# A two-layer block on one Trainium2 core: the delta rule's inverse in blocks of 64, and four other moves in the order of the work

## The chip, the core and the metric

The kernel runs on one core of one Trainium2 chip. The metric is the device time of one execution in microseconds (us), lower is better. Before the change three runs took 820.45, 818.7 and 819.86 us; the median is 819.86 us.

## What is computed

Two layers are applied to x of shape (1, 256, 1024) in fp32. The first holds a Mamba-2 branch (SSD), an RG-LRU branch and a feed-forward part with a depthwise convolution; the second has four branches (gated delta rule, spatial gating, sliding window, attention to a memory of 256 tokens), each gated and projected up. The parts that the change touches are these, cut from the reference:

```python
# RG-LRU gates, 16 blocks of 64 channels
r = sigmoid(einsum("bshi,hij->bshj", xb, wr) + br)
i = sigmoid(einsum("bshi,hij->bshj", xb, wi) + bi)
# memory branch: the memory is normed, then projected to keys and values
mem_kv = _rmsnorm(mem, norm_mem) @ w_mem_kv
# delta rule: q and k with unit length, 4 heads of 128
q = _l2norm(q) * (DN_DK ** -0.5); k = _l2norm(k)
L = where(strict, einsum("bhncd,bhnsd->bhncs", kb, k) * exp(diff), 0.0)
sol = triangular_solve(eye + L, rhs, left_side=True, lower=True, unit_diagonal=True)
```

The reference solves in chunks of 64 tokens; the kernel works in chunks of 128, so that there are 2 chunks x 4 heads = 8 unit triangular matrices of 128 x 128 to be inverted.

## The kernel before

**Products.** All activations lie with channels or tokens on the 128 partitions, 256 tokens wide. Every fp32 weight comes from HBM in pieces of 128 x 1024 (512 KB) that SyncE's queue streams through three raw buffers. ScalarE rounds a piece to `whi` (L112), VectorE computes the rest `wlo` (L113), and TensorE makes each product from three matmuls: high by high, low by high, high by low (`mm3`, L419 to L421; `proj_wide`, L457). In the first products of all, `ly`, the activations themselves are also being split while they are used: `HU` on ScalarE (L616), `LU` on VectorE (L617).

**The order.** TensorE, ScalarE and VectorE run what the program's order gives them. Class `Weave` (L146) makes the order: a main generator walks through the big projections and yields after each small unit of matmuls; side generators hold everything else. A side's `yield n` asks for n units of the main work before it goes on, `yield ("event", n)` asks for n units after a named event, and a plain string in the main work joins a side: what is left of it is then emitted at once. In the first layer's gate and merge projections a unit is 3 x 2 matmuls of 128x512. TensorE executes strictly in that order, so whatever is placed too early makes TensorE wait. Instructions inside `tc.high_priority()` are moved ahead on ScalarE and VectorE.

**Places that the change touches.**
- The LRU gates `pg` (L804): after part p of the projection `lx` the convolution leaves `XC`; half of it, the channels of the odd blocks, is copied by a DMA of GpSimd's queue to `XW` (L1030) so that all blocks lie on partitions 0 to 63. The gates of part p are issued 10 units after `lx{p}`.
- The memory (`prm`, L924): the norms of the memory tokens are spread over the partitions by two matmuls, ScalarE copies them to `MEM` (L927), GpSimd scales the transposed memory `MT` in four operations (L932), ScalarE rounds each half to `EH` (L934), VectorE makes the rest `EL` (L935). All that runs beside the projections `pb` and `o`; `m1b` (L962) transposes the merged branches into `MH` and `ML` (L965, L966), which `o` reads.
- The norms of q and k (`pss`, L1270; `psst`, L1279): two sets of matmuls, with a copy `ss` on VectorE (L1274) between them.
- The inverse. `diagonal()` (from L1238) sends the 32 x 32 diagonal blocks through a DRAM tensor `dl` so that they lie with (matrix, block) on the partitions, and GpSimd does the forward substitution for 32 blocks at once: 31 steps of a product (L1250) and a subtraction (L1254), 128 x 248 elements in the first and 128 x 8 in the last. The results go back through `dx`. Then, 44 units later, two levels of merges on TensorE turn blocks of 32 into 64 and 64 into 128: per level and chunk four matmuls `pit` (L1344), four transposes `piy` (L1353) and four matmuls `pix` (L1362, L1364).
- `delta` is joined by the main work just before the merge of branch 3; `G2` (gates of a branch) and `MG2` (their sum) have separate buffers.

Of the kernel before, what the change touches and what calls it, by code (L numbers as in the profile page):

```python
# [8 lines left out]
F32 = mybir.dt.float32  # L9
# [187 lines left out]
def two_blocks_kernel(  # L197
# [11 lines left out]
    lvl: bass.AP,  # L209
# [153 lines left out]
    def small_proj(o, hh, hl, a, n, nm):  # L363
# [9 lines left out]
        nc.vector.tensor_copy(f, pf[:, 0:S])  # L373
        yield 5
# [8 lines left out]
    def rows(o, src, nm, wait):  # L383

        n = src.shape[2]
        cat = sm.tile([P, 2, P], F32R, tag="cat", name=f"{nm}_cat", bufs=1)
        nc.gpsimd.memset(cat.bitcast(F32), 0.0)
        split(cat[:, :, 0:n], cat[:, :, n : 2 * n], src)
# [4 lines left out]
        nc.vector.tensor_copy(o, pT[:, 0:S])  # L393
# [508 lines left out]
    def side_mem():  # L902
# [18 lines left out]
        yield 8  # L921
# [23 lines left out]
    class Merged:  # L945
# [11 lines left out]
        def turn(self, tt, c):  # L957
            yield 4 if self.nm == "m1" else 3
# [177 lines left out]
    def block2(HH, HL, HX, MK, MV):  # L1136
        lws = big.tile([P, 16, P], F32, tag="b8", name="lws")
        wst = lws[:, 0:4, :]
        lvs = lws[:, 4:9, :].rearrange("p a c -> p (a c)")
        lv = lvs[:, 0:448].rearrange("p (l c) -> p l c", l=7)  # L1140
        lv0 = lvs[:, 448:576]
# [10 lines left out]
        nc.sync.dma_start(lvs[:, 0:576], lvl)  # L1152
# [17 lines left out]
        XI = [bXY[:, 0], bXY[:, 1]]  # L1170
        YI = [bXY[:, 2], bXY[:, 3]]

# [10 lines left out]
        def side_decay():  # L1183
# [3 lines left out]
            nc.scalar.activation(beta, ba[:, :, 0:4], AF.Sigmoid)  # L1187
            nc.vector.tensor_tensor(
                out=gg, in0=ba[:, :, 4:8],
                in1=row("dt_bias_2").unsqueeze(1).to_broadcast([P, 2, 4]), op=ALU.add)  # L1190
            ggf = gg.rearrange("p t h -> p (t h)")
            softplus(ggf, ggf, 8, "spdn")
            nc.vector.scalar_tensor_tensor(
                gg, in0=gg, scalar=-1.0, in1=ea2.unsqueeze(1).to_broadcast([P, 2, 4]),
                op0=ALU.mult, op1=ALU.mult)
# [4 lines left out]
            nc.vector.tensor_copy(gc, pgc[:, 0:12])  # L1200
            gcT = sm.tile([P, S], F32R, name="gcT", bufs=1)
            nc.vector.tensor_tensor(out=kds, in0=gc[:, 8:12], in1=gc[:, 0:4], op=ALU.subtract)
            nc.scalar.activation(kds, kds, AF.Exp)
            nc.scalar.activation(e1, gc[:, 4:8], AF.Exp)
            nc.vector.tensor_scalar(neg1, e1, -1.0, None, op0=ALU.mult)
            yield from rows(gcT, gc[:, 0:8].rearrange("p (c h) -> p c h", c=2), "pgT", 9)
            yield 2
            for c in range(2):
# [5 lines left out]
                for h in range(4):  # L1214
                    nc.scalar.activation(EE[c][:, h, :], pe[:, h * P : (h + 1) * P], AF.Relu,
                                         scale=-1.0, bias=gc[:, 4 * c + h : 4 * c + h + 1])
                nc.scalar.activation(EE[c], EE[c], AF.Exp, scale=-1.0)
# [3 lines left out]
                yield 1  # L1221

        sqs = {}

        def diagonal():

            LA8 = bLA[:, 0:2].rearrange("p c h l -> p (c h) l")
            XI8 = bXY[:, 0:2].rearrange("p c h l -> p (c h) l")
            dl = dp.tile([8, 4, 32, 32], F32, name="dl")
            dx = dp.tile([8, 4, 32, 32], F32, name="dx")  # L1230

            lb = bXY[:, 2:4].rearrange("p a h (b l) -> p (a h b) l", l=32)
            xb = bM[:, 0:256].rearrange("p (i k) -> p i k", k=8)
            ta = bM[:, 256:512].rearrange("p (i k) -> p i k", k=8)
            eng = nc.gpsimd
            for b in range(4):
                r = slice(32 * b, 32 * b + 32)
                eng.dma_start(dl[:, b].rearrange("c s l -> s c l"), LA8[r, :, r])  # L1238
            eng.memset(XI8, 0.0)
            eng.memset(xb, 0.0)  # L1240
            for g in range(4):
                q = slice(32 * g, 32 * g + 32)
                eng.affine_select(out=xb[q], in_=xb[q], compare_op=ALU.not_equal, fill=1.0,
                                  base=-8 * g, pattern=[[1, 32], [-1, 8]],
                                  channel_multiplier=0)
                eng.dma_start(lb[q], dl.rearrange("c b s l -> (c b) s l"))
            for j in range(31):
                n = 31 - j
                t = ta[:, 0:n, :]
                eng.tensor_tensor(  # L1250
                    out=t, in0=xb[:, j : j + 1, :].to_broadcast([P, n, 8]),
                    in1=lb[:, j, j + 1 : 32].unsqueeze(2).to_broadcast([P, n, 8]),
                    op=ALU.mult)
                eng.tensor_tensor(out=xb[:, j + 1 : 32, :], in0=xb[:, j + 1 : 32, :], in1=t,  # L1254
                                  op=ALU.subtract)
            for g in range(4):
                eng.dma_start(
                    dx[:, :, :, 8 * g : 8 * g + 8].rearrange("c b i k -> (c b) i k"),
                    xb[32 * g : 32 * g + 32])
            for b in range(4):  # L1260
                r = slice(32 * b, 32 * b + 32)
                eng.dma_start(XI8[r, :, r], dx[:, b].rearrange("c i k -> i c k"))

        def side_delta():

            for a in range(2):
                yield (f"dn{a}1", 10)
                pss = bank(f"pss{a}")
                for h in range(4):
                    nc.tensor.matmul(pss[32 * h : 32 * h + 32, 0:S], one[:, 0:32],  # L1270
                                     sqs[a, h // 2][:, h % 2, :], start=True, stop=True,
                                     tile_position=(0, 32 * h))
                f = sm.tile([P, S], F32, tag="spf", name=f"ss{a}", bufs=1)
                nc.vector.tensor_copy(f, pss[:, 0:S])  # L1274
                yield 3
                pst = bank(f"psst{a}")
                for tt in range(2):
                    t = slice(tt * P, (tt + 1) * P)
                    nc.tensor.transpose(pst[:, t], f[:, t], ident)  # L1279
                nc.vector.tensor_copy(  # L1280
                    rn[:, a], pst[:, 0:S].rearrange("p (t h c) -> p t h c", t=2, c=32)[:, :, :, 0])


            sk, rq = rn[:, 0], rn[:, 1]
            nc.scalar.activation(sk, sk, AF.Sqrt, bias=eps1)
            nc.scalar.activation(rq, rq, AF.Sqrt, bias=epsq, scale=128.0)
            nc.vector.reciprocal(rq, rq)
            nc.vector.reciprocal(wk, sk)
            nc.vector.tensor_tensor(out=wk, in0=wk, in1=wk, op=ALU.mult)
            nc.vector.tensor_tensor(out=wk, in0=wk, in1=beta, op=ALU.mult)  # L1290
# [13 lines left out]
            yield 1  # L1304
# [3 lines left out]
            for c in range(2):  # L1308
                t = slice(c * P, (c + 1) * P)
                for p in range(2):  # L1310
# [5 lines left out]
                    for j in range(2):  # L1316
                        h = 2 * p + j
                        nc.vector.scalar_tensor_tensor(
                            LT[c][:, h, :], in0=pk[:, j * S : j * S + P],
                            scalar=wk[:, c, h : h + 1], in1=EE[c][:, h, :],  # L1320
                            op0=ALU.mult, op1=ALU.mult)
                    e = EE[c][:, 2 * p : 2 * p + 2, :]
                    nc.vector.tensor_tensor(out=e, in0=v2(pk)[:, :, P:S], in1=e, op=ALU.mult)
# [3 lines left out]


            diagonal()
            yield 44  # L1330

            def even(ap, l):
                return ap.rearrange("p (b a i) -> p b a i", a=2, i=1 << l)[:, :, 0, :]

            def even4(ap, l):
                return ap.rearrange("p h (b a i) -> p h b a i", a=2, i=1 << l)[:, :, :, 0, :]

            Ts = [None, None]
            for l in range(5, 7):
                for c in range(2):  # L1340
                    pt = bank(f"pit{l}{c}")
# [570 lines left out]
```

## Time and profile before

| | |
|---|---|
| runs | 818.7, 819.86, 820.45 us (median 819.86) |
| the profiled execution | 822.88 us, of which the span from its first to its last instruction is 821.2 us |
| TensorE (PE) busy | 804.1 us, 98% of the span; mean granted clock 0.997 |
| VectorE (DVE) busy | 612.9 us, 75% |
| ScalarE (ACT) busy | 526.8 us, 64% |
| GpSimd (POOL) busy | 67.5 us, 8% |
| DMA | 147.63 MB, 180 GB/s over the span |

The profile is of one execution, which took 3.0 us longer than the median of the runs. Engines run side by side, so that the busy shares do not add up; the chain of work that ended last says which of them set the end, and the list of waits says where TensorE stood still. "a x4" in a row stands for four instructions in a row of the same kind; an fp32 product that is not split shows as two matmuls in the trace, so that "x8" are four products.

### The profile page before, as it was taken

How to read it: one execution, taken by the hardware profiler on the slowest of the kernel's cores; microseconds unless marked ns; L12 is line 12 of the kernel's file. 1: busy time of each engine (PE TensorE's matmuls, PEld its weight loads, DVE VectorE, ACT ScalarE, POOL GpSimd, SP SyncE). 2: the span in 40 equal slices, each digit the busy share in tenths (PEclk: the TensorE clock that was granted, in tenths of full speed). 3: DMA queues.
4: the chain of work that ended last, by engine and by line, in shares of the span. 5: the costliest groups of instructions: out<-in, count | busy, mean ns of one | idle time of the engine just before them, and what ended most of it. 6: DMA issues, size and time to landing. Idle time of an engine off the chain costs nothing.

```text
span 821.2 us, 13190 instructions
## 1 busy us (share of the span) xinstructions
PE 804.1 (98%) x4978; PEld 708.2 (86%) x4978; DVE 612.9 (75%) x1017; ACT 526.8 (64%) x830; POOL 67.5 (8%) x113
## 2 busy tenths in 40 slices
PE   6999999899999999999999999999999999999997
PEld 6999887688879999999988889888888888888886
DVE  5899799888688788888744687877786657566583
ACT  7585998895656656565644378955976555544452
POOL 0000001000200000000000100029830000000000
PEclk9999999999999999999999999999999999999999
DMA  8655456466754655555566554543554445655651
GB/s 317 204 206 172 133 168 209 152 217 229 262 171 135 222 188 180 185 175 198 195 199 201 185 166 146 188 150 107 175 148 148 137 145 169 194 192 190 199 185 52
DMA packets 41631, 147.63 MB, mean 180 GB/s; under 512 B 5024, under 2 KB 5280, under 8 KB 41568
## 3 DMA queue, kind: packets, MB, share of 16 engines
q1 hardware_dynamic: 40464, 144.82, 52.3%
q0 software_dynamic: 960, 1.97, 1.1%
q8 instruction: 39, 0.64, 0.3%
q14 instruction: 24, 0.20, 0.1%
q10 hardware_dynamic: 144, 0.00, 0.0%
HBM read 144.42 MB, written 1.31 MB: 177 GB/s over the span
## 4 chain that ended last, share of the span: by engine, by line
PE 92%; DVE 5%; DMA 2%; ACT 1%; issue 0%; DVEq 0%; SPq 0%; ACTq 0%; POOLq 0%
PE z L457 8%; PE fu L421 6%; PE fu L420 6%; PE fu L419 6%; PE g L419 5%; PE g L420 5%; PE g L421 5%; PE fd L421 3%; PE fd L420 3%; PE fd L419 3%; PE lx L457 2%; PE up L421 2%; PE up L419 2%; PE up L420 2%; PE o L421 1%; PE xbc L419 1%
## 5 line engine op out<-in xcount | busy, mean ns | idle before, releaser
L113 DVE TENSOR_TENSOR wlo<-wraw,whi 128x1024 fp32r<-128x1024 f32 x256 | 312.6, 1227 | 132.3 <-ACT whi L112 129.6
L112 ACT CAST whi<-wraw 128x1024 fp32r<-128x1024 f32 x256 | 267.3, 1050 | 192.0 <-PE fu L420 48.1
L419 PE MATMUL fu<-HX,whi 128*128 128x256 f32 x384 | 108.7, 283 | 0.0
L420 PE MATMUL fu<-HX,whi 128*128 128x256 f32 x384 | 108.7, 283 | 0.0
L421 PE MATMUL fu<-HX,wlo 128*128 128x256 f32 x384 | 108.7, 283 | 0.0
L419 PE MATMUL g<-whi,HX 128*128 128x512 f32 x192 | 76.3, 397 | 0.0
L420 PE MATMUL g<-wlo,HX 128*128 128x512 f32 x192 | 75.3, 392 | 0.0
L421 PE MATMUL g<-whi,HX 128*128 128x512 f32 x192 | 75.2, 392 | 0.0
L419 PEld LDWEIGHTS fu<-HX,whi 128*128 128x128 f32 x384 | 73.7, 192 | 0.0
L420 PEld LDWEIGHTS fu<-HX,whi 128*128 128x128 f32 x384 | 73.7, 192 | 0.0
L421 PEld LDWEIGHTS fu<-HX,wlo 128*128 128x128 f32 x384 | 73.7, 192 | 0.0
L457 PE MATMUL z<-HX,whi 128*128 128x512 f32 x192 | 69.7, 400 | 0.0
L457 PE MATMUL z<-HX,wlo 128*128 128x256 f32 x192 | 51.3, 288 | 0.0
L599 DVE SCALAR_TENSOR_TENSOR fc<-fu,pc,fc 128x255 f32<-128x255 f32 (+1 forms) x96 | 43.7, 478 | 1.6
L419 PEld LDWEIGHTS g<-whi,HX 128*128 128x128 f32 x192 | 36.3, 189 | 8.6 <-issue 1.1
L421 PEld LDWEIGHTS g<-whi,HX 128*128 128x128 f32 x192 | 36.3, 189 | 7.7
L420 PEld LDWEIGHTS g<-wlo,HX 128*128 128x128 f32 x192 | 36.4, 189 | 7.2
L457 PEld LDWEIGHTS z<-HX,whi 128*128 128x128 f32 x192 | 35.6, 188 | 6.4 <-issue 0.3
L457 PEld LDWEIGHTS z<-HX,wlo 128*128 128x128 f32 x192 | 36.3, 189 | 2.1 <-issue 0.5
L419 PE MATMUL fd<-whi,FH 128*128 128x512 f32 x96 | 37.4, 389 | 0.0
L420 PE MATMUL fd<-wlo,FH 128*128 128x512 f32 x96 | 37.4, 389 | 0.0
L421 PE MATMUL fd<-whi,FL 128*128 128x512 f32 x96 | 37.3, 389 | 0.0
(533 smaller groups left out, 1890.4 us busy)
## 6 DMA issues: line engine op xcount, KB each, us to landing
wraw<-in_w_in_dram SPq DMA_DIRECT2D x130, 512.0 KB, 3.4
wraw<-in_w_fu_dram SPq DMA_DIRECT2D x48, 512.0 KB, 3.6
wraw<-in_w_fd_dram SPq DMA_DIRECT2D x24, 512.0 KB, 3.6
wraw<-in_w_o_dram SPq DMA_DIRECT2D x16, 512.0 KB, 4.1
wraw<-in_w_up_dram SPq DMA_DIRECT2D x16, 512.0 KB, 3.3
wraw<-in_w_pa_dram SPq DMA_DIRECT2D x8, 512.0 KB, 4.1
wraw<-in_w_pb_dram SPq DMA_DIRECT2D x8, 512.0 KB, 4.3
wraw<-in_w_mk_dram SPq DMA_DIRECT2D x4, 512.0 KB, 4.4
```

What stands on the lines that cost most here:

```text
L112: nc.scalar.copy(hi, raw)
L113: nc.vector.tensor_tensor(out=lo, in0=raw, in1=hi.bitcast(F32), op=ALU.subtract)
L419: nc.tensor.matmul(o, wh, xh, start=first, stop=False)
L420: nc.tensor.matmul(o, wh, xl, start=False, stop=False)
L421: nc.tensor.matmul(o, wl, xh, start=False, stop=last)
L457: nc.tensor.matmul(*p, start=k + i == 0, stop=k == 7 and i == 1)
L599: nc.vector.scalar_tensor_tensor(o[:, d:S], in0=p[:, 0 : S - d], scalar=col(wname, (taps - 1 - d) * n + i), in1=o[:, d:S], op0=ALU.mult, o ...
```

## The change

1. **Blocks of 64.** `diagonal()` goes. GpSimd now inverts the 16 diagonal blocks of 64 x 64 (`unit`, `blocks_out`, `rows_in`, `forward`, `blocks_in`): 63 steps of a product and a subtraction, on 128 partitions that hold (column residue mod 8, block). The first 16 of these operations are on one column group of up to 63 elements, the longest are on 128 x 156. Rows of the blocks come in four portions of eight DMAs on GpSimd's own queue, placed among the steps. One merge is left on TensorE: 8 transposes of 64 x 64 (`pix0`), 8 products of 64 x 64 (`pit`), 8 more (`pix1`), with copies on ScalarE and VectorE between. It is due 72 units after the event `inv`. The table `lvl` and its DMA go.
2. **The norms apart.** The norm of k comes first (`norms(0)`, 10 units after `dn01` as before), that of q after the blocks have been handed to GpSimd. The products k·k and k·q (`pkk`) no longer wait for `dn21`. Short VectorE and ScalarE operations of this side work run with high priority.
3. **Products on zeros.** VectorE clears 128 x 384 elements of `NRM` at the very start, and six 128x256 fp32 products on them (`pw`) stand ahead of TensorE's first work.
4. **Memory.** `prm` is due 15 units instead of 8 after the norms, `m1` takes a unit less between its pieces.
5. **LRU gates.** `pg` is due 12 units after `lx{p}` instead of 10.
6. **Buffers.** `G2` of branch 3 is summed in place, the other branches' `G2` lies in buffer `b3`, `delta` is joined one branch later.

```diff
-            yield (f"lx{p}", 10)
+            yield (f"lx{p}", 12)
...
-        yield 8
+        yield 15
         ps = bank("prm")
...
-            yield 4 if self.nm == "m1" else 3
+            yield 3
...
+        def rows_in(i):
+            for g in range(8):
+                q, r = slice(16 * g, 16 * g + 16), slice(16 * i, 16 * i + 16)
+                if i < 2:
+                    o, c = lb0[q, r], slice(0, 64)
+                else:
+                    o, c = lb1[q, 16 * i - 32 : 16 * i - 16], slice(32, 64)
+                nc.gpsimd.dma_start(o, dl[:, :, r, c].rearrange("c b s l -> (c b) s l"))
+        def forward(js):
+            eng = nc.gpsimd
+            for j in js:
+                a, n = j // 8 + 1, 63 - j
+                t = bM[:, 1792 : 1792 + a * n].rearrange("p (k i) -> p k i", k=a)
+                l = lb0[:, j, j + 1 : 64] if j < 32 else lb1[:, j - 32, j - 31 : 32]
+                eng.tensor_tensor(
+                    out=t, in0=xb[:, 0:a, j : j + 1].to_broadcast([P, a, n]),
+                    in1=l.unsqueeze(1).to_broadcast([P, a, n]), op=ALU.mult)
+                x = xb[:, 0:a, j + 1 : 64]
+                eng.tensor_tensor(out=x, in0=x, in1=t, op=ALU.subtract)
...
-            for a in range(2):
-                yield (f"dn{a}1", 10)
...
+            yield ("dn01", 10)
+            yield from norms(0)
...
+            yield ("E", 1)
+            yield ("dn11", 6)
...
+            blocks_out()
+            rows_in(0)
+            forward(range(4))
+            rows_in(1)
+            forward(range(4, 16))
+            wv.event("inv")
+            yield from norms(1)
...
+            yield ("inv", 8)
+            forward(range(16, 20))
+            rows_in(2)
+            forward(range(20, 32))
+            rows_in(3)
+            forward(range(32, 63))
+            blocks_in()
             yield ("dn21", 7)
...
-            diagonal()
-            yield 44
...
+            yield ("inv", 72)
+            X0 = bXY[0:64, 0:2].rearrange("p c h l -> p (c h l)")[:, 0:512]
+            T = tmp("T")[64:P]
+            px = bank("pix0")
+            for i in range(8):
+                nc.tensor.transpose(px[0:64, i * 64 : (i + 1) * 64], YI8[0:64, i, 0:64],
+                                    ident[0:64, 0:64])
+            nc.scalar.copy(X0, px[0:64])
+            yield 3
...
-                yield "delta"
-                MG = big.tile([P, 2, D], F32, tag="b3", name="MG2")
+                MG = G2
...
             elif n == 2:
+                yield "delta"
...
+            nc.vector.memset(NRM[:, 0:384], 0.0)
+            pw = bank("pw")
+            for _ in range(6):
+                nc.tensor.matmul(pw[:, 0:S], NRM[:, 0:P], NRM[:, P : P + S], start=True, stop=True)
```

How the change moves instructions shows at three places. The first is TensorE around the last part's LRU gates `pg`, beside the gate projection `g`; `pg` from `XW` is what needs the copied half. Before, `pg` follows the first two units of `g`'s column block `g_00_1776`:

```order
L419 MATMUL g_00_1776<-whi_1670,HX_102 128x512
L420 MATMUL g_00_1776<-wlo_1671,HX_102 128x512
L421 MATMUL g_00_1776<-whi_1670,HX_102 128x512
L804 MATMUL pg_1796<-XC,lw 64x256
L804 MATMUL pg_1797<-XW,lw 64x256
```

After the change the same gates (`pg_1843`, `pg_1844`) stand behind twelve more matmuls of `g` and behind the eight small `pgr`:

```order
L586 MATMUL pgr<-ident2r,gnrh 128x128
L588 MATMUL pgr<-ident2r,gnrl 128x128
L421 MATMUL g_10_1785<-whi_1678,HX_102 128x512
L422 MATMUL g_10_1785<-wlo_1679,HX_102 128x512
L423 MATMUL g_10_1785<-whi_1678,HX_102 128x512
L421 MATMUL g_10_1785<-whi_1678,HX_102 128x512
L422 MATMUL g_10_1785<-wlo_1679,HX_102 128x512
L423 MATMUL g_10_1785<-whi_1678,HX_102 128x512
L806 MATMUL pg_1843<-XC,lw 64x256
L806 MATMUL pg_1844<-XW,lw 64x256
```

So `pgr`, which came after the gates, now comes before them, and the gates come twelve matmuls and these eight later.

The second place is ScalarE in the projection `o`, where `EH` is the rounded scaled memory, `MH` the rounded merged branches, and `whi` a rounded weight piece. Before, eight `EH` stand ahead of the last two `MH`, which `o` needs at once:

```order
L965 CAST MH<-m1b_2360 128x4x128
L112 CAST whi_2412<-wraw_2336 128x1024
L927 COPY MEM<-prm 128x256
L112 CAST whi_2418<-wraw_2342 128x1024
L965 CAST MH<-m1b_2403 128x4x128
L934 ACTIVATE EH<-MT,pc 128x256 x8
L554 ACTIVATE warm<-eps_99 128x1
L112 CAST whi_2460<-wraw_2410 128x1024
L112 CAST whi_2466<-wraw_2416 128x1024
L965 CAST MH<-m1b_2482 128x4x128
L112 CAST whi_2510<-wraw_2458 128x1024
L965 CAST MH<-m1b_2501 128x4x128
```

After the change:

```order
L112 CAST whi_2450<-wraw_2400 128x1024
L967 CAST MH<-m1b_2460 128x4x128
L929 COPY MEM<-prm 128x256
L936 ACTIVATE EH<-MT,pc 128x256 x3
L967 CAST MH<-m1b_2503 128x4x128
L936 ACTIVATE EH<-MT,pc 128x256 x5
L112 CAST whi_2518<-wraw_2442 128x1024
L112 CAST whi_2524<-wraw_2448 128x1024
```

The last `MH` now stands behind three `EH` only; the weight pieces `whi_2518` and `whi_2524` of `o`'s second half stand behind all eight.

The third place is GpSimd at the start of the inverse: the blocks go out to `dl`, come back as rows, and the steps begin. Before:

```order
L1238 DMA dl<-bLA 32x8x32 x4
L1246 DMA bXY<-dl 32x1024 x4
L1250 TENSOR_TENSOR bM<-bM,bXY 128x248
L1254 TENSOR_TENSOR bM<-bM 128x248
L1250 TENSOR_TENSOR bM<-bM,bXY 128x240
L1254 TENSOR_TENSOR bM<-bM 128x240
```

After the change:

```order
L1258 DMA dl<-bLA 64x8x64 x2
L1268 DMA lb_5143<-dl 16x1024 x10
L1277 TENSOR_TENSOR bM<-bM,lb_5143 128x63
L1268 DMA lb_5143<-dl 16x1024
L1281 TENSOR_TENSOR bM<-bM 128x63
L1268 DMA lb_5143<-dl 16x1024
L1277 TENSOR_TENSOR bM<-bM,lb_5143 128x62
L1268 DMA lb_5143<-dl 16x1024
L1281 TENSOR_TENSOR bM<-bM 128x62
```

Ten row DMAs are issued ahead of the first step, and one more between each two operations until all are out; the steps are shorter in the beginning and there are twice as many.

## Rows read from the trace of the kernel before

**Rows 1.** The page, the chain that ended last, shares of the span by engine.
```profile
PE 92%; DVE 5%; DMA 2%; ACT 1%; issue 0%; DVEq 0%; SPq 0%; ACTq 0%; POOLq 0%
```
**Rows 2.** Waits of TensorE: line and releaser, us in total, times, longest.
```profile
PE pg L804 <- DMA XW<-XC: 2.1, 1, 2.1
PE o L421 <- DVE ML L966: 1.1, 1, 1.1
PE psst L1279 <- DVE ss L1274: 0.9, 1, 0.9
```
**Rows 3.** Timeline of TensorE, the start: start us, duration us, instruction, [idle before].
```profile
6.71 0.58 PE L419 MATMUL ly<-HU,whi 128*128 128x256 f32 x1 [6.71 <-ACT HU L616]
...
10.81 0.38 PE L421 MATMUL ly<-HU,wlo 128*128 128x256 f32 x1
11.03 0.29 PE L419 MATMUL ly<-HU,whi 128*128 128x256 f32 x1
...
19.08 0.68 PE L628 MATMUL prx<-ident,rx 128*128 128x128 f32 x4
```
**Rows 4.** Timeline of VectorE, the operation that makes prx's operand.
```profile
18.78 0.16 DVE L1764 RECIPROCAL rx<-rx 128x2 f32<-128x2 f32 x1
```
**Rows 5.** Timeline of TensorE at the last part's LRU gates.
```profile
146.70 0.40 PE L804 MATMUL pg<-XW,lw 64*64 64x256 f32 x1 [2.06 <-DMA XW<-XC]
```
**Rows 6.** Busy time by stretch behind these gates (PE, PEld, DVE, ACT, POOL, PEclk, DMA).
```profile
148.00:150.00 2.00, 2.00 (x5) 1.48 (x5) 1.18 (x3) 1.98 (x5) 0.00 (x0) 0.50 0.73 252
```
**Rows 7.** The chain at these gates, in order of time: start us, us, what.
```profile
141.94 4.63 DMA XW<-XC
...
146.70 1.59 PE pg L804 x12
...
149.02 0.43 PE g L420
```
**Rows 8.** Timeline of TensorE, the memory norms.
```profile
218.99 0.60 PE L924 MATMUL prm<-ident,rm 128*128 128x128 f32 x4
```
**Rows 9.** Timeline of GpSimd, the scaling of the memory.
```profile
220.59 7.17 POOL L932 TENSOR_TENSOR MT<-MT,MEM 128x512 f32<-128x512 f32 x4 [77.62 <-ACT MEM L927]
```
**Rows 10.** Timeline of ScalarE, the last two roundings of the memory.
```profile
227.79 0.91 ACT L934 ACTIVATE EH<-MT,pc 128x256 fp32r<-128x256 f32 x2 [0.52 <-POOL MT L932]
```
**Rows 11.** The chain at the merges, in order of time.
```profile
625.27 0.84 PE pit L1344 x8
626.11 0.44 PE piy L1353 x4
626.55 2.79 PE z L457 x16
...
642.42 0.60 PE pit L1344 x8
643.02 0.59 PE piy L1353 x4
...
652.84 0.23 PE g L420
```
**Rows 12.** Timeline of TensorE, the last products k·k and k·q.
```profile
541.07 1.03 PE L1314 MATMUL pkk<-KQ 128*128 128x256 f32 x4
```
**Rows 13.** Timeline of GpSimd: three steps of the substitution, and the way back.
```profile
557.30 0.70 POOL L1254 TENSOR_TENSOR bM<-bM 128x240 f32<-128x240 f32 x1
...
561.65 1.53 POOL L1254 TENSOR_TENSOR bM<-bM 128x216 f32<-128x216 f32 x1
...
596.24 0.20 POOL L1250 TENSOR_TENSOR bM<-bM,bXY 128x8 f32<-128x8 f32 x1
...
605.02 2.33 POOL L1262 DMA_DIRECT2D bXY<-dx  x4 [4.89 <-DMA dx<-bM]
```
**Rows 14.** Timeline of VectorE beside the second of these steps.
```profile
561.35 1.31 DVE L113 TENSOR_TENSOR wlo<-wraw,whi 128x1024 fp32r<-128x1024 f32 x1
```

More of the change, by code (lines that the diff above doesn't have):

```diff
@@ L372, in small_proj @@
         f = sm.tile([P, S], F32, tag="spf", name=f"{nm}_f", bufs=1)
-        nc.vector.tensor_copy(f, pf[:, 0:S])
-        yield 5
+        with tc.high_priority():
+            nc.vector.tensor_copy(f, pf[:, 0:S])
+        yield 3
         ps = bank(f"{nm}t")
@@ L387, in rows @@
         nc.gpsimd.memset(cat.bitcast(F32), 0.0)
-        split(cat[:, :, 0:n], cat[:, :, n : 2 * n], src)
+        with tc.high_priority():
+            split(cat[:, :, 0:n], cat[:, :, n : 2 * n], src)
         yield wait
@@ L392, in rows @@
             nc.tensor.transpose(pT[:, tt * P : (tt + 1) * P], cat[:, tt].bitcast(F32), ident)
-        nc.vector.tensor_copy(o, pT[:, 0:S])
+        with tc.high_priority():
+            nc.vector.tensor_copy(o, pT[:, 0:S])
     def softplus(o, v, n, nm):
@@ L1186, in side_decay @@
             yield from small_proj(ba, HH, HL, baab[0], 8, "psb")
[L1187 to L1195, printed above, removed]
+            with tc.high_priority():
+                rates()
             yield 9
@@ L1199, in side_decay @@
             nc.tensor.matmul(pgc[:, 8:12], one, gg[:, 0, :], start=True, stop=True)
-            nc.vector.tensor_copy(gc, pgc[:, 0:12])
+            with tc.high_priority():
+                nc.vector.tensor_copy(gc, pgc[:, 0:12])
             gcT = sm.tile([P, S], F32R, name="gcT", bufs=1)
[L1202 to L1206, printed above, removed]
+            yield from rows(gcT, gc[:, 0:8].rearrange("p (c h) -> p c h", c=2), "pgT", 5)
             yield 2
@@ L1213, in side_decay @@
                                      gcT[:, c * P : (c + 1) * P], start=True, stop=True)
[L1214 to L1217, printed above, removed]
+                with tc.high_priority():
+                    for h in range(4):
+                        nc.scalar.activation(
+                            EE[c][:, h, :], pe[:, h * P : (h + 1) * P], AF.Relu,
+                            scale=-1.0, bias=gc[:, 4 * c + h : 4 * c + h + 1])
+                    nc.scalar.activation(EE[c], EE[c], AF.Exp, scale=-1.0)
                 nc.gpsimd.affine_select(
@@ new lines, in block2, with unit @@
+        sqs = {}
+        dl = dp.tile([8, 2, 64, 64], F32, name="dl")
+        dy = dp.tile([8, 2, 64, 64], F32, name="dy")
+        lb0 = big.tile([P, 32, 64], F32, tag="b1", name="lb0")
+        lb1 = bXY[:, 0:2].rearrange("p c h (a l) -> p (c h a) l", l=32)
+        def unit():
+            eng = nc.gpsimd
+            eng.memset(YI8, 0.0)
+            eng.memset(xb, 1.0)
+            for sign in (1, -1):
+                eng.affine_select(
+                    out=xb, in_=xb, compare_op=ALU.is_ge, fill=0.0,
+                    base=15 if sign > 0 else 0, pattern=[[-128 * sign, 8], [16 * sign, 64]],
+                    channel_multiplier=-sign)
@@ L1235, in diagonal, with blocks_out @@
+        def blocks_out():
+            LA8 = bLA[:, 0:2].rearrange("p c h l -> p (c h) l")
             eng = nc.gpsimd
-            for b in range(4):
-                r = slice(32 * b, 32 * b + 32)
+            for b in range(2):
+                r = slice(64 * b, 64 * b + 64)
                 eng.dma_start(dl[:, b].rearrange("c s l -> s c l"), LA8[r, :, r])
[L1239 to L1246, printed above, removed]
@@ new lines, in blocks_in, with norms @@
+        def blocks_in():
+            eng = nc.gpsimd
+            for g in range(8):
+                eng.dma_start(
+                    dy.rearrange("c b (k g) i -> g (c b) k i", g=8)[g],
+                    xb[16 * g : 16 * g + 16])
+            for b in range(2):
+                r = slice(64 * b, 64 * b + 64)
+                eng.dma_start(YI8[r, :, r], dy[:, b].rearrange("c k i -> k c i"))
+        def norms(a):
+            pss = bank(f"pss{a}")
+            for h in range(4):
+                nc.tensor.matmul(pss[32 * h : 32 * h + 32, 0:S], one[:, 0:32],
+                                 sqs[a, h // 2][:, h % 2, :], start=True, stop=True,
+                                 tile_position=(0, 32 * h))
+            f = sm.tile([P, S], F32, tag="spf", name=f"ss{a}", bufs=1)
+            with tc.high_priority():
+                nc.vector.tensor_copy(f, pss[:, 0:S])
+            yield 3
+            pst = bank(f"psst{a}")
+            for tt in range(2):
+                t = slice(tt * P, (tt + 1) * P)
+                nc.tensor.transpose(pst[:, t], f[:, t], ident)
+            with tc.high_priority():
@@ L1303, in side_delta @@
                                         op=ALU.mult)
[L1304 to L1310, printed above, removed]
-                    pk = bank(f"pkk{c}{p}")
-                    for j in range(2):
-                        h = 2 * p + j
-                        nc.tensor.matmul(pk[:, j * S : (j + 1) * S], KQ[:, h, 0, t],
-                                         KQ[:, h, :, t], start=True, stop=True)
[L1316 to L1323, printed above, removed]
-                    yield 1
@@ new lines, in side_delta @@
+                yield 1
+            yield ("inv", 72)
[6 more added lines that the diff above has]
+            nc.scalar.copy(X0, px[0:64])
+            yield 3
+            pt = bank("pit")
+            for i in range(8):
+                nc.tensor.matmul(pt[64:P, i * 64 : (i + 1) * 64], LT[i // 4][0:64, i % 4, 64:P],
+                                 X0[:, i * 64 : (i + 1) * 64], start=True, stop=True)
@@ L1377, in solve @@
+            nc.scalar.activation(T, pt[64:P], AF.Copy, scale=-1.0)
+            yield 3
+            px = bank("pix1")
+            for i in range(8):
+                nc.tensor.matmul(px[0:64, i * 64 : (i + 1) * 64], T[:, i * 64 : (i + 1) * 64],
+                                 YI8[64:P, i, 64:P], start=True, stop=True)
+            nc.vector.tensor_copy(YI8[0:64, :, 64:P],
+                                  px[0:64].rearrange("p (c l) -> p c l", c=8))
+            yield 3
             def solve(c):
@@ L1697, in block2 @@
                 wv.add("y0", branch0())
-            G2 = big.tile([P, 2, D], F32, tag="b1", name=f"G2{n}")
+            G2 = big.tile([P, 2, D], F32, tag="b1" if n == order[0] else "b3", name=f"G2{n}")
             for c in range(2):
@@ L1788 @@
 _ARGS = (
[L1789 removed]
+    "x", "xT", "mem", "memT", "pcol", "prow", "wsm", "lruw", "wsT", "post", "gbias", "w_in", "w_pa", "w_pb",
     "w_o", "w_mk", "w_mv", "w_fu", "w_fd", "w_in2", "w_up2", "w_o2",
@@ L1879, in _layout @@
     d["wsT"] = np.ascontiguousarray(a("spatial_w_2")[0].transpose(2, 0, 1)).reshape(P, 4 * P)
-    i = np.arange(P)
-    lv = []
-    for l in range(7):
-        b = i >> l
-        m = np.where((b[:, None] % 2 == 1) & (b[None, :] == b[:, None] - 1), -1.0, 0.0)
-        lv.append(m[:, b % 2 == 0])
-        if l == 0:
-            m0 = m.T
-    d["lvl"] = np.concatenate(lv + [m0], axis=1).astype(np.float32)
     return {k: np.ascontiguousarray(d[k]) for k in _ARGS}
```

136 lines of the change are left out of this document (47 added, 89 removed).

## The prediction

> **What bounds the kernel now.** I read the chain that ended last first: TensorE holds 92% of it [rows 1], so a change counts only where TensorE waits, runs at half clock, or is given less to do. The list of its waits comes next. Beside the unavoidable start it holds three that the change touches: 2.1 us for the copied half `XW` of the LRU gates, 1.1 for `ML` in `o`, 0.9 for the copy `ss` in the norms [rows 2]. Then the timelines at these places, for what a wait costs beyond itself, and the chain at the merges, for the work that falls away. Everything below is a difference to the profiled execution of 822.88 us, which lies 3.0 above the median of 819.86; I take the differences off the median. About 0.2%, or 1.6 us, is what a measurement of this kernel can tell from no change.
>
> **LRU gates, -4.1 us.** The last gates stand still for 2.06 us until 146.70 [rows 5], because the DMA to `XW` was issued at 141.94 and needs 4.63 us, landing at 146.57 [rows 7]. It is not only that: behind the wait the granted clock falls to 0.50, the lower level of 1.2 GHz [rows 6]. The twelve gate records take 1.59 us and a matmul of `g` 0.43 [rows 7], where one at full clock takes 0.23 [rows 11]. Six of them pass before the clock is back, 6 x 0.20 = 1.2, and the gates themselves lose about half, 0.8. Wait and clock are 4.1 us. After the change the gates come behind twelve more matmuls of `g`, 12 x 0.23 = 2.8 us, and behind the eight `pgr`. Without the wait the first that reads `XW` would have run at 146.70 - 2.06 = 144.6; now it is due at 147.4, and some 0.8 later still for `pgr`. `XW` lands at 146.57 if its producer is not moved, so 0.8 to 1.6 us are to spare. What hides it is `g`, whose weights are already split by then. Bounds: nothing if `XC` comes two microseconds later, 4.3 if all goes.
>
> **Memory and `o`, -0.3 us.** The 1.1 us for `ML` [rows 2] go, since only three `EH` stand ahead of its `MH` on ScalarE. No clock fell behind this wait. But something else is now late: `whi_2518` and `whi_2524` stand behind all eight `EH`, and these are paced by GpSimd's four scalings, 7.17 us [rows 9]. In the trace the last `EH` is done 227.79 + 0.91 - 218.99 = 9.7 us after `prm` [rows 8, 10]. The piece of weight then needs a rounding and a subtraction, 1.0 and 1.3 us [rows 14] (that row is a subtraction; the rounding takes a little less), so its low half is there 11.6 us after `prm`, with some overlap 11.3. In the new order 43 matmuls of `o` at 0.23 and the last `m1b` stand between `prm` and the first that reads this low half, 10.5 us. So a new wait of 0.8 takes the place of 1.1; bounds 0 and 2.0, since each EH and copy may run half a microsecond either way.
>
> **Norms, -0.9 us.** The copy `ss` gets high priority and 3 units are time enough; the 0.9 [rows 2] go. Bounds 0.4 and 0.9: what it now overtakes on VectorE, a weight's subtraction, may be waited for by `dn`.
>
> **Merges, -4.7 us.** In the chain, `pit` and `pix` of the level of 32 are four blocks of 0.84, `piy` 0.44 and 0.45; of the level of 64 four blocks of 0.60 and two `piy` of 0.59 [rows 11] (one of each stands there). Together 3.36 + 0.89 + 2.40 + 1.18 = 7.8 us. What replaces them: two groups of eight 64 x 64 products, each twice a block of 0.60, 2.4 us; and eight transposes of 64 x 64, which the trace does not show. Four of 128 x 128 took 0.44, so eight lie between 0.44 (half the columns, half the time) and 0.88 plus a change of work; I take 0.7, as their columns count. 7.8 - 3.1 = 4.7, with bounds 4.3 and 5.2. The copies between them lie beside three units of `z` or `g`, 1 to 2 us, and cost nothing unless these engines are late. Weight `lvl`, 288 KB, goes from SyncE's queue and frees nothing that is waited for.
>
> **Products on zeros, -0.1 us.** The first 18 matmuls of `ly` come every 0.21 us, at half rate, later ones every 0.12 [rows 3] (the slow ones lie between 6.71 and 11.03). Six products of 128x256 fp32 before them would run while TensorE is idle: two take 0.68 at full clock [rows 12] (1.03 with the last one's drain), so at half clock six take 4.1 us, up to 6.2, and begin after a clear of about 0.3 at 1 us. They end at 5.4 to 7.5, against 6.71; I take no delay. If the clock is then full, 18 x 0.09 = 1.6 us are won, until TensorE reaches `prx`. That started at 19.08, and its operand was ready at 18.94 [rows 3, 4], by a chain of roundings and squares on ScalarE that nobody shortens. So 0.1 remains and the rest becomes a wait there. Bounds +0.8 and -1.6. The Trainium skill, "TensorE: Matmul & The Clock Gate", section "Why this matters for your kernels", says to keep TensorE busy from the start to get past the slow level; that the first matmuls are slow agrees with these rows, and by the rule alone the term would be the full 1.6.
>
> **GpSimd, 0 if in time.** This is what the merges wait for. Before, 62 operations with 3968 elements per partition of each kind: a step costs 0.18 + 0.0022 n us from 0.70 at 240 and 0.20 at 8 elements [rows 13], 62 x 0.18 + 2 x 3968 x 0.0022 = 28.6, and they ran from about 554 to 597, 42.5 us with the gaps. The rest are steps like that of 1.53 where its size calls for 0.65, next to a weight's subtraction on VectorE of 1.31 [rows 13, 14]. Ratio 1.49. After: 126 operations, 6384 elements of each kind, 126 x 0.18 + 2 x 6384 x 0.0022 = 50.8, times 1.49 is 76 us. Of the 32 row DMAs ten lie ahead of the first step, 22 among the steps, each 0.58 us of issue as the four of 2.33 [rows 13], 13 us. Ahead, from the last `pkk` to the first step 15 us as before [rows 12, 13] (541.07 to some 554, and six more issues); behind, ten issues and two landings of at most 4.9 [rows 13], 15.6. Sum 120 us. What PE has meanwhile: 625.27 - 541.07 = 84 us in the trace [rows 11, 12]. By the order, 136 matmuls of 128x512 and 64 of 128x256 more stand between; a pair of `z` costs 2.79 / 8 = 0.35 [rows 11] and `g` 0.23, so 64 x 0.35 + 72 x 0.23 = 39 us; the second norm and the transposes of k and v, now in between too, some 3. Sum 126. The merge is due 6 us after the blocks are back, by a sum whose parts may be off by 10.
>
> **Buffers, 0.** `G2` waits for `b3` only where q and k are long read; `delta` has a branch more of time.
>
> **Sum.** -4.1 - 0.3 - 0.9 - 4.7 - 0.1 = -10.1 us: 812.8 for an execution like the profiled one, **809.8 us** against the median.
>
> **Rivals.**
> *Part is given back* (0.19). The wait for `XW` stays because its producer is moved as well, or the new wait in `o` grows from 0.8 past 2 us and brings the fall of clock that followed 2.06 us at the gates: 4.1 back, or 1.2 + 2.0 = 3.2. 813 to 814. For it: both margins are about 1 us. Against: in neither case does the work that must come first grow.
> *GpSimd is some microseconds late* (0.11). Its margin of 6 is smaller than what the sum may be off; TensorE waits 2 to 10 us at `pix0`. 812 to 820, 0.06 of it still faster, 0.05 no change to be seen.
> *GpSimd decides* (0.08), the other side. 13 of the 62 steps before were stretched by about 0.9 [rows 13]. Twice as many, shorter steps, each with a chance to run into a subtraction with two operands from SBUF: if every second one is hit, 63 x 0.9 = 57 instead of the 25 us that are in the sum, 32 more, less the margin of 6, less 10 gained elsewhere: 16 slower, 836. It decides from 16 us of further stretch on. Against: VectorE's subtractions come at the pace of the weights, so hits go with time, not with the number of steps. The Trainium skill, "GPSIMD Engine Reference", section "Key points", has GpSimd share its SBUF interfaces with VectorE, with contention where VectorE reads two operands from SBUF, and calls VectorE about twice as fast for elementwise work; the stretched step beside `wlo` agrees, and by this rule the work should not have been doubled here.
> *The start gives all* (0.04). If `prx`'s operand comes earlier as well, the full 1.6: 808.3. Against it, the row at 18.78.
>
> **How the numbers follow.** The forecast itself, 807.8 to 811.5 us, has 0.58. Faster by over 0.2% is 0.58 + 0.19 + 0.06 + 0.04 = 0.87; no change 0.05; slower 0.08. The range is 807.0 to 815.5: below, the bounds of `o` and the merges and part of the start; above, the part given back. Out of it are the late GpSimd cases, 0.17.
>
> **What would show it.** Right: no row `pg <- DMA XW` among TensorE's waits and no stretch of clock 0.50 near 147 us; no `psst`; at most a wait of about 1 us at `o`, for `wlo` and no longer for `ML`; two groups of 1.2 us and one of 0.7 in place of the merges; `ly` at 0.12 from the start and a wait of some 1.5 us at `prx`. Wrong: a wait of TensorE at `pix0` for the blocks, which would make the sum worth as much less, or `ly` still every 0.21 us.

## The result, and the profile after

The changed kernel takes 813.21 us in the median (813.11, 813.21, 813.21, 814.86); before, on the same chip, 819.93 (818.7 to 820.45). The ratio is 0.9929, with an interval of 0.9915 to 0.9942: 6.7 us faster, where 10.1 were forecast. The time lies inside the range of 807.0 to 815.5, but 3.4 us above the forecast, and the reason is not one of size alone.

The two profiled executions do differ by what was forecast: 822.88 against 813.11 us is 9.8. So the sum came close for that pair of executions, in part by luck, as the account below shows. It did not describe the median, because the execution profiled before was slower than every other one of that kernel that was measured: the others lie between 818.6 and 820.9 us.

The waits of TensorE in the changed kernel (line and releaser, us in total, times, longest) answer to [rows 2]:

```profile
PE pw L1786 <- DVE eps L318: 1.4, 1, 1.4
PE m1b L964 <- DVE MG L1078: 1.0, 1, 1.0
PE ly L421 <- ACT HU L618: 1.0, 1, 1.0
PE prx L630 <- DVE rx L1797: 0.4, 1, 0.4
PE o L423 <- DVE ML L968: 0.4, 1, 0.4
PE ly L423 <- DVE wlo L113: 0.4, 1, 0.4
PE mk L423 <- DVE wlo L113: 0.2, 1, 0.2
```

`XW` and `ss` are gone, `ML` has shrunk from 1.1 to 0.4. New is 1.0 us for `m1b`. The waits of 0.4 for a weight at `ly` and for `rx` at `prx` take back what the start won. The timeline of TensorE at the start, beside [rows 3]:

```profile
1.39 4.34 PE L1786 MATMUL pw<-NRM 128*128 128x256 f32 x12 [1.39 <-DVE eps L318]
6.71 0.38 PE L421 MATMUL ly<-HU,whi 128*128 128x256 f32 x1 [0.98 <-ACT HU L618]
...
13.88 0.39 PE L423 MATMUL ly<-HU,wlo 128*128 128x256 f32 x1 [0.42 <-DVE wlo L113]
...
19.03 0.68 PE L630 MATMUL prx<-ident,rx 128*128 128x128 f32 x4 [0.45 <-DVE rx L1797]
```

The products on zeros end at 5.73 and `ly` starts at the same 6.71 as before; `prx` starts at 19.03, before at 19.08. The matmuls between run at 0.12 us from the fourth on, so 1.5 us are won by 9.3 us, and by 19 all but less than 0.1 us is given back.

The merge in the chain of the changed kernel, beside [rows 11]:

```profile
656.53 0.57 PE pix L1387 x8
...
661.40 1.07 PE pit L1393 x16
...
666.78 1.07 PE pix L1399 x16
```

2.7 us in place of 7.8. And GpSimd's timeline, beside [rows 13] (the first step, two neighbours of almost equal size, the last step, and the way back):

```profile
544.31 0.29 POOL L1277 TENSOR_TENSOR bM<-bM,lb 128x63 f32<-128x63 f32 x1 [1.44 <-DMA lb<-dl]
...
592.13 0.46 POOL L1281 TENSOR_TENSOR bM<-bM 128x136 f32<-128x136 f32 x1
592.66 1.28 POOL L1277 TENSOR_TENSOR bM<-bM,lb 128x132 f32<-128x132 f32 x1
...
640.10 1.15 POOL L1281 TENSOR_TENSOR bM<-bM 128x8 f32<-128x8 f32 x1
641.55 4.21 POOL L1287 DMA_DIRECT2D dy<-bM  x8 [0.30 <-POOL bM L1281]
648.99 1.39 POOL L1292 DMA_DIRECT2D bXY<-dy  x2 [3.23 <-DMA dy<-bM]
```

The steps with the row DMAs among them take 544.31 to 641.25, 97 us. The last two DMAs need about 4.2 us from issue to landing, so the blocks are back between 653 and 654, some 3 us before `pix` at 656.53.

### The profile page after: what moved, and what is told of

It is laid out like the page before. It is cut to its first block, busy times and chain, and to the rows that moved or that the text cites. A ratio compares the mean times of both kernels' runs of the same rounds, so it can differ in the third digit from the quotient of the medians.

```text
span 811.4 us, 13224 instructions
## 1 busy us (share of the span) xinstructions
PE 800.2 (99%) x4950; PEld 703.6 (87%) x4950; DVE 613.1 (76%) x1011; ACT 528.9 (65%) x831; POOL 117.7 (15%) x203
## 4 chain that ended last, share of the span: by engine, by line
PE 85%; DVE 6%; DMA 3%; ACT 3%; issue 2%; POOL 0%; DVEq 0%; SPq 0%; ACTq 0%
PE z L459 8%; PE fu L423 6%; PE fu L422 6%; PE fu L421 6%; PE g L421 5%; PE g L422 4%; PE g L423 4%; PE lx L459 3%; PE fd L423 3%; PE fd L422 3%; PE fd L421 3%; PE up L421 2%; PE up L422 2%; PE up L423 2%; DVE wlo L113 2%
## 5 line engine op out<-in xcount | busy, mean ns | idle before, releaser
L1281 POOL TENSOR_TENSOR bM<-bM 128x56 f32<-128x56 f32 (+47 forms) x63 | 38.2, 607 | 4.2
```

The source lines that it names most:

```text
L1281: eng.tensor_tensor(out=x, in0=x, in1=t, op=ALU.subtract)
```

## The experiments

Each was timed against the kernel before on the same chip; that one's median was 819.7 to 819.9 us in all of them.

**The kernel before once more.** No edit.

> The kernel before, unchanged, profiled and timed once more. Theory A (the profiled execution of before, 822.88 us, was an unusual one: it lost 4 us at the LRU gates by the late XW and the half clock, which ordinary executions of 819.9 us lose only in part): most executions at 819 to 820.5 us with a mean granted clock of 0.998 to 0.999, a slower one shows 0.997; a profile of an ordinary execution has no stretch at clock 0.50 behind the gates, or a wait under 1 us there. Theory B (every execution loses the 4 us at the gates, and the 3 us lie elsewhere): the same wait of about 2 us and the same stretch at 0.50 in this profile, whatever its time.

Measured: 819.99 us in the median, 819.22 to 820.81, ratio 1.000 (0.9992 to 1.0009). The profiled execution took 819.22 us. Its waits of TensorE:

```profile
PE ly L419 <- ACT HU L616: 6.8, 1, 6.8
PE o L421 <- DVE ML L966: 1.1, 1, 1.1
PE psst L1279 <- DVE ss L1274: 0.9, 1, 0.9
PE mv L420 <- DVE wlo L113: 0.2, 1, 0.2
```

The wait for `XW` is not among them. Busy time by stretch (PE, PEld, DVE, ACT, POOL, PEclk, DMA), the stretch of [rows 6]:

```profile
148.00:150.00 2.00, 2.00 (x11) 1.68 (x11) 2.00 (x5) 1.99 (x3) 0.00 (x0) 1.00 0.97 373
```

The clock is full, and 11 matmuls pass where 5 did. The DMA view of this stretch has the cause: issue to landing of the two halves of `XW`, KB each and the median in us, in this profile

```profile
XW<-XC POOLq DMA_DIRECT2D x2, 128.0 KB, 3.1
```

and in the first profile of the same kernel

```profile
XW<-XC POOLq DMA_DIRECT2D x2, 128.0 KB, 4.5
```

This transfer took 1.4 us longer and was issued 0.75 us later in the first profile (141.94 against 141.19); the later issue comes down from a weight that landed later (ScalarE's rounding of it began at 137.57 against 136.83). In this one the gates can go on. With the two traces of before laid side by side, matmul by matmul, the first loses 3.8 us at this one place and nothing else over 0.2: 2.1 at the wait, 0.5 at the gates behind it, 1.2 at the matmuls that follow. The clock did not fall at once; two stretches of the first profile show it (columns as above), the wait ending at 146.70:

```profile
146.00:147.00 1.00, 0.30 (x6) 0.30 (x10) 1.00 (x1) 0.00 (x0) 0.00 (x0) 1.00 0.60 147
147.00:148.00 1.00, 1.00 (x14) 0.41 (x10) 0.10 (x1) 0.08 (x1) 0.00 (x0) 0.78 0.96 381
```

Of the 61 other executions of this kernel whose clock is on record none shows a mean granted clock below 0.998, against 0.997 for the one profiled first. Theory A stands; why the transfer was slow there is not shown.

**Only the gates moved.** `10` to `12` in the kernel before:

```diff
-            yield (f"lx{p}", 10)
+            yield (f"lx{p}", 12)
```

> The kernel before with the LRU gates 12 units behind their projection instead of 10, nothing else. Theory A: 0.5 to 1.5 us less than before in the median (819.9 to about 819). Theory B: 4 us less, about 815.8.

Measured: 821.43 us (818.73 to 823.47), ratio 1.0021 (1.0010 to 1.0032). Slower, which neither theory had. Two rows of its profile say how, the wait of `o` and the stretch behind it:

```profile
PE o L421 <- DVE ML L966: 2.1, 1, 2.1
```

```profile
232.00:234.00 2.00, 1.57 (x6) 1.24 (x7) 2.00 (x3) 0.02 (x1) 0.00 (x0) 0.84 0.88 272
234.00:236.00 2.00, 2.00 (x6) 1.63 (x5) 1.05 (x2) 1.02 (x1) 0.00 (x0) 0.50 0.93 285
236.00:238.00 2.00, 2.00 (x8) 1.60 (x8) 0.97 (x2) 0.69 (x2) 0.00 (x0) 0.81 0.85 246
```

The gates' own place gains 0.6 us against the second profile of before; then `o` waits 2.1 instead of 1.1 us, the clock falls to 0.50 behind it, and 3 us are lost. The memory's loads go out at 203.97 instead of 202.14 and land more slowly (6.5 against 5.7 us), its norms come 2.5 us later on ScalarE and with them the scaling and the roundings in front of `MH`. That the later gates caused the later load is argued from this, not shown. Of the ten executions six show a mean granted clock of 0.996 and take 821.0 to 823.5 us; the other four, at 0.998 and 0.999, take 818.7 to 821.4.

**The change with the gates back at 10.**

```diff
-            yield (f"lx{p}", 12)
+            yield (f"lx{p}", 10)
```

> The changed kernel with the LRU gates back at 10 units. Theory A: 0.5 to 1.5 us more than the change (813.2 to about 814.2), with single executions 3 to 4 us above the others where the clock falls. Theory B: 4 us more, about 817.3, in every execution.

Measured: 813.26 us (812.98 to 813.9), the change's own 813.21. In the traces the gates at 12 win 1.1 us where they stand (sixteen matmuls in 1.02 us instead of 2.1: with `XW` there, the first four start within 0.03 us of each other), and the new wait of 1.0 us at `m1b` takes them back: with the gates at 10 that wait does not exist, and the same piece of `m1b` runs at 215.66, in the change at 215.63.

**The change without the products on zeros.**

```diff
-            nc.vector.memset(NRM[:, 0:384], 0.0)
-            pw = bank("pw")
-            for _ in range(6):
-                nc.tensor.matmul(pw[:, 0:S], NRM[:, 0:P], NRM[:, P : P + S], start=True, stop=True)
```

> The changed kernel without the six products on zeros. The prediction's term: 0.1 us more than the change, with ly at 0.21 us apart in the beginning and no wait at prx. Rival (the start gives all): 1.5 us more. Second rival (the products cost, since they hold the first ly): 0 to 0.8 us less.

Measured: 814.68 us (813.61 to 815.86), 1.5 above the change. In its profile 0.6 us are lost up to `prx`, of which 0.24 are a later start of `ly`; another 0.75 at `m1b`, which now waits twice, 1.6 us in all.

**Only the products on zeros, in the kernel before** (the same four lines added).

> The kernel before with the six products on zeros, nothing else. The prediction's term: 0.1 us less than before, with ly at 0.12 us apart and a wait of up to 1.5 us at prx. By the pair with and without them on the changed kernel (813.2 and 814.7): 1.5 us less. By the positions in those two traces at the matmul after prx: 0.4 to 0.6 us less.

Measured: 819.81 us (819.16 to 820.55), ratio 1.0002 (0.9993 to 1.0011). Nothing, as the prediction had it: `ly` runs at 0.12 us and the waits at `ly` (0.6) and `prx` (0.5) eat it. The 1.5 us of the pair above are thus not the start's own.

**The change with the memory as before.**

```diff
-        yield 15
+        yield 8
...
-            yield 3
+            yield 4 if self.nm == "m1" else 3
```

> The changed kernel with the memory branch as before: its scaling due 8 units after the norms instead of 15, m1 one unit later. Theory C (the gates at 12 units delay the memory's chain, so that the wait of o for ML grows past 2 us and the clock falls behind it, as in the kernel before with the gates alone; the later scaling is what prevents it): about 816, with a wait of 2 us or more at o and a stretch at clock 0.50 behind it. The prediction's term: 0.3 us more than the change, 813.5, with a wait of 1.1 us for ML and a clock of 1.00.

Measured: 814.0 us, with executions from 812.62 to 818.26, ratio 0.9938 (0.9920 to 0.9956). The profile is that of the fastest: `o` waits 1.7 us, the clock stays full, `m1b` does not wait. So it is between both expectations. The median is 0.8 above the change's, the intervals overlap; what is plain is that the executions lie further apart. That the long ones are those with a fallen clock is likely after the run with the gates alone: the longest, 818.26, shows a mean granted clock of 0.996, the two fastest 0.999. None of the long ones was profiled.

**Only the inverse, the norms and the buffers.** Zeros out, gates at 10, memory as before, all edits as above.

> Only the inverse, the norms and the buffers: the changed kernel without the products on zeros, with the gates at 10 units and the memory as before. The prediction's terms, 4.7 + 0.9 = 5.6 us less than before: 814.3. By the aligned traces of before (its second profile) and after, these two parts are 5.0 + 0.9: 814.0. If instead the whole 6.7 us are theirs and the three other moves cancel: 813.2.

Measured: 813.74 us (813.44 to 814.5), ratio 0.9931 (0.9919 to 0.9943): 5.95 us less than before. No run parts the norms from the merges; that is read from the traces below.

**The same with the products on zeros.**

> The inverse, the norms, the buffers and the products on zeros; gates at 10 units and the memory as before. If the moves of the gates and of the memory are worth nothing together (their gains at one place are waits at the next): 813.2, as the change. If they are worth the prediction's 4.1 + 0.3: 817.6. If they cost: 812.5.

Measured: 813.26 us (812.13 to 813.44), ratio 0.9917 (0.9904 to 0.9931). The whole change has 813.21. So the moves of the gates and of the memory, for which 4.4 us were forecast, are together worth nothing that can be measured.

**The merge sooner.**

```diff
-            yield ("inv", 72)
+            yield ("inv", 64)
```

> The changed kernel with the merge due 64 units after inv instead of 72, so 8 units of g, 10.9 us, sooner. By the trace of the change GpSimd's blocks are back 3.5 us before the merge: a wait of about 7.4 us at pix0 and a fall of the clock behind it worth some 2 us, together 820 to 823. If the margin were 10 us or more: no wait, 813.

Measured: 825.9 us (822.32 to 827.22), ratio 1.0071 (1.0053 to 1.0089). The wait and the stretch around it:

```profile
PE pix L1387 <- DMA bXY<-dy: 7.5, 1, 7.5
```

```profile
650.00:655.00 5.00, 1.83 (x10) 1.59 (x11) 0.00 (x0) 0.70 (x2) 0.76 (x2) 0.50 0.42 146
```

10.9 us sooner makes a wait of 7.5: the margin of the change is 3.4 us. The profiled pair differs by 9.2 us, so what comes behind the wait, the half clock above all, costs about 1.8 more. The unprofiled executions lose 3 to 5 us more than that, at mean granted clocks of 0.990 to 0.993 against 0.994.

**Two attempts at something better.** First, the reciprocal of the memory's norms taken from PSUM after they are spread, and the first two pieces of `m1` a unit later:

```diff
-        nc.vector.reciprocal(rm, rm)
         yield 15
...
-        nc.scalar.copy(rmb, ps[:, 0:S])
+        nc.vector.reciprocal(rmb, ps[:, 0:S])
...
-            yield 3
+            yield 4 if self.nm == "m1" and c == 0 else 3
```

> The changed kernel with the two waits of the memory's place taken away: the reciprocal of the memory's norms is taken after they are spread (VectorE, from PSUM, in place of ScalarE's copy) so that VectorE no longer stops for it, and the first two pieces of m1 come one unit later again. Theory: the waits at m1b (1.0 us) and at o (0.4 us) go, 1.0 to 1.4 us less than the change, 811.8 to 812.2. Rival: something else waits there next (a weight's low half), less than 0.3 us won.

Measured: 815.47 us (814.34 to 820.16), ratio 0.9957 (0.9942 to 0.9971), worse than the change. Both waits went as meant (1.7 us ahead of the change by 235 us), and two others came:

```profile
PE n_t L529 <- DVE o_or L498: 2.5, 1, 2.5
...
PE pix L1386 <- DMA bXY<-dy: 1.1, 1, 1.1
```

The transposes `n_t` of the residual norm wait 2.5 us, because TensorE gets there 1.7 us sooner while their operand on VectorE comes 0.7 us later (`o_or` at 251.85 against 251.11); and here GpSimd's last step ends at 645.5 instead of 641.25, so its margin is gone too.

Second, only the later pieces of `m1`:

```diff
-            yield 3
+            yield 4 if self.nm == "m1" and c == 0 else 3
```

> The changed kernel with the first two pieces of m1 one unit later, nothing else. Theory: the wait of 1.0 us at m1b (VectorE makes MG behind a weight's subtraction that waits for ScalarE) goes and nothing else is late: 812.2 in executions like the profiled one. Rival: the inverse on GpSimd has no room, TensorE comes to pix0 a microsecond earlier and waits there: 813.2.

Measured: **812.1 us** (811.91 to 812.43), ratio 0.9907 (0.9893 to 0.9920), every execution below every one of the change, though the intervals of the two ratios still touch (the change's begins at 0.9915). In the profile `m1b` no longer waits. Why it did shows in VectorE's timeline of the change:

```profile
212.71 0.17 DVE L922 RECIPROCAL rm<-rm 128x2 f32<-128x2 f32 x1 [1.62 <-ACT rm L921]
212.80 0.67 DVE L1077 TENSOR_TENSOR G<-pb,G 128x512 f32<-128x512 f32 x1
213.66 1.23 DVE L113 TENSOR_TENSOR wlo<-wraw,whi 128x1024 fp32r<-128x1024 f32 x1 [0.19 <-ACT whi L112]
214.80 0.68 DVE L1078 TENSOR_TENSOR MG<-MG,G 128x512 f32<-128x512 f32 x1
```

`MG` stands behind a reciprocal and a weight that both wait for ScalarE, which is squaring the memory there; TensorE's transpose runs at 215.63. The change brought `m1b` a unit forward, into this, and the gates at 12 units brought TensorE there 1.1 us sooner; either taken back alone removes the wait.

**The same with 4 units more for GpSimd** (`72` to `76`).

> The same with the merge due 76 units after inv, so that GpSimd has 5.4 us more. If single executions wait at pix0 (the blocks came 3.5 us early in the profile of the change, 1.1 us late in that of the version with the reciprocal in another place): the executions lie closer together and the median is 0 to 0.8 us below the one with 72. If GpSimd is always in time: equal to it.

Measured: 812.48 us (812.14 to 813.05), ratio 0.9911 (0.9898 to 0.9925), not better than with 72. Its profile has 1.4 us of wait at `m1b` again, but at another piece. The second, where the change waits, goes without a wait here (215.89) as in the run above (216.11). The fourth waits, because its `MG` took 1.77 us on VectorE where it takes 0.68 in the change, beside GpSimd's scaling of the memory, which had just begun:

```profile
226.16 6.10 POOL L934 TENSOR_TENSOR MT<-MT,MEM 128x512 f32<-128x512 f32 x4 [83.09 <-ACT MEM L929]
226.49 1.77 DVE L1078 TENSOR_TENSOR MG<-MG,G 128x512 f32<-128x512 f32 x1
228.41 0.63 PE L964 MATMUL m1b<-ident,MG 128*128 128x128 f32 x4 [1.39 <-DVE MG L1078]
```

In the change this `MG` begins at 225.73 and the scaling at 227.24, so they do not meet. How often they meet in other executions is not shown.

## Why the prediction was right or wrong

**The LRU gates, -4.1: wrong, and this is the step that failed.** The wait and the clock did cost about what was set in that execution, 3.8 us, though not split as set: the gates lost 0.5 and not 0.8, since the clock fell only some 0.9 us after the wait had ended. But the prediction said the execution lay 3.0 us above the median and then took "the differences off the median", as if that excess were spread evenly. It sat in this one place. In the second profile of before the gates do not wait and the clock does not fall. What 12 units win is 0.6 us there, and 0 in the time, because `m1b` and `o` come next. Moved alone they cost 1.5 us.

**Memory and `o`, -0.3: too small to show in the time, and wrong in the trace.** The 1.1 us became 0.4. It was still `ML` that was waited for, while the weight behind the eight `EH`, for which 0.8 was set, was in time: the four scalings took 5.4 us instead of the 7.17 of [rows 9], with no subtraction of a weight beside them in VectorE's timeline. What was overlooked is the last edit of this part, `m1` a unit sooner: with the gates at 12 it makes 1.0 us of wait at `m1b`, so that by these two waits the part costs 0.3 us where 0.3 was to be won. The prediction costed what was removed there and not that a step moved forward needs its operand sooner. Laid over the second trace of before, the change is 0.12 us ahead at the first `ly` and 0.16 at 477 us, behind `o`, `mk` and `mv`: what the start, the gates and the memory won and lost up to there comes to nothing.

**Norms, -0.9, and merges, -4.7: right.** 5.6 forecast; the two with the buffers alone gave 5.95 (the trace of that run also gains 0.5 us at `mv` and loses 0.8 at the gates). In the aligned traces 1.0 us falls at the norm and 5.0 at the merges. The transposes took 0.57 (0.7 set), the products 1.07 for each group of eight (1.2 set), 2.7 instead of 3.1.

**Products on zeros, -0.1: right.** 0.0 in the kernel before. (The prediction speaks of half clock at the start; the profile's clock column reads 1.00 there even while the first `ly` come every 0.21 us, so the slow start is read from this spacing alone.) The rival by which the whole 1.6 would stay fell: `prx` starts at 19.03.

**GpSimd in time: right, with less room.** 15 us from the last `pkk` (at 529.4) to the first step, as set; 97 us of steps and DMAs, 89 set; the way back about 12, 15.6 set. Margin about 3 us by the trace and by the merge made sooner, 6 set. Of the steps 30 in 126 took over 0.5 us more than their size asks for (0.18 + 0.0022 n), 11 in 62 before, where the prediction had counted 13: a quarter, not half as in the rival that ended slower. Of the 27 steps that began while VectorE was in a weight's subtraction 25 are among the stretched, of the other 99 five; and per us of steps the hits are nearly as frequent as before (30 in 97 us, 11 in 42.5), so they go with time, as the prediction argued against that rival. What a late GpSimd costs shows with the merge 10.9 us sooner: the kernel is 0.7% slower than before. The Trainium skill, "GPSIMD Engine Reference", section "Key points", on contention with VectorE over SBUF agrees with these stretched steps; here it decided over the margin, not over the sign.

**The sum for the profiled pair.** Its 9.8 us against 10.1 are partly luck. Aligned, the gates gave 4.4 (3.8 of the first profile's loss and the 0.6), the norm 1.0 and the merges 5.0, together some 0.8 more than set; from there to 477 us the memory, `o` and what follows lost 0.7 where 0.3 was to be won.

**The chance.** "Part is given back" had 0.19 and is what happened, at 813.2 of its 813 to 814. Not by its words, though: `XW` no longer waits, and `o` did not grow. Most of the part was never there to win, and the rest was lost at `m1b`.

## What to carry to other kernels

Where the profiled execution lies above the runs, look for the place where the excess sits before any term is taken off the median; a wait that ends on a DMA is the first suspect, and a second profile of the unchanged kernel answers it. A step that is moved needs two costs: what waits for it, and what it now waits for. And where an engine in order is 98% busy, a wait removed early in a stage is worth only what the next wait in that stage leaves: here the moves of the gates, the memory and the start came to nothing together, and one unit at the next wait was worth about 1.1 us.

## What the runs showed of the hardware that was not expected

Gaps of nearly the same length did not end alike. Behind 2.06 us (before, first profile) and 2.13 (gates alone) the granted clock was 0.50, the level of 1.2 GHz, for some 3 us, from about 0.9 us after TensorE had gone on; in the wait of 7.45 (merge sooner) it was 0.50 from 650 us, still within the wait, and full again from 657, 4 us behind its end. Behind 2.47 us at `n_t` it stayed at 2.4 GHz, in the stretch that follows that wait:

```profile
252.00:254.00 2.00, 1.91 (x17) 1.00 0.00 0
```

(The columns here are PE, PEclk, the DMA's share and GB/s.) Behind 1.70 (memory as before), 1.39 (the last run), 1.10 and 0.93 (before) it stayed too. Why 2.06 and 2.47 end differently is not shown. The Trainium skill, "TensorE: Matmul & The Clock Gate", section "Why this matters for your kernels", warns of idle gaps between bursts of matmuls; the runs agree in that all three falls came behind such a gap, but two of these gaps are shorter than the ones that it warns of, and here the measurement decides. A price for a gap near 2 us has to hold both outcomes. Eight products of 64 x 64 also ran faster in one group of eight (1.07 us) than in two groups of four (2 x 0.60), and sixteen 64-row gate matmuls took 1.02 us together but 2.1 when half of them had to wait for their operand.
